# Five of eight coefficient batches on GpSimd, and a scan whose tables and products share one psum bank

## The chip, the cores and the metric

The kernel runs on one core of one Trainium2 chip. The metric is device time in microseconds (us) for one execution. Five engines matter here, each with its own in-order queue: TensorE (PE), VectorE (DVE), ScalarE (ACT), GpSimd (POOL) and SyncE (SP, which only issues DMAs). Lines such as L312 are lines of the kernel before.

## The reference, cut to what matters

Two layers of an encoder over 512 tokens of width 1024. The first layer mixes tokens with a bidirectional diagonal state-space model, the second with a short convolution; each layer then attends to 256 memory tokens and applies a squared-ReLU MLP. The part that the change touches is the state-space mixer of layer 0 and, beside it, the keys and values of layer 0's memory:

```python
u = h @ w_in                                  # 64 groups of 16 channels
for r in range(2):                            # two directions
    a_bar = exp(lam * dt)                     # 64 complex states per group
    bu = einsum('gph,lbgh->lbgp', b_bar, u)
    states = associative_scan(a_bar * left + right, bu)
    y = y + einsum('ghp,lbgp->blgh', c, states).real
z = gelu(y); z = z * sigmoid(z @ w_glu); out = z @ w_out
k, v = split(m @ w_kv)                        # memory keys and values, independent of the scan
```

## The kernel before

The tokens are cut into 64 chunks (`NC`) of 8. Inside a chunk the recurrence is a small matrix product; between chunks a scan of 63 steps carries the state. The mixer is written out by hand (`manual_schedule`): on each engine the instructions stand in the order in which the source issues them. The rest of the kernel, from about 238 us on, is left to a scheduler.

The steps of the mixer that matter here, in the order of the source:

- `s_mats(b)` (L522 to L531): TensorE makes the chunk inputs of 8 groups, ScalarE copies them into `estate`. The last of these copies must land before the scan begins, since every scan step uses all 64 groups.
- `q_ops(b)` (L535, by way of `gen_ops`, L466): five VectorE products and sums of 128x1024 that make one of eight batches `Q[b]` of the table C a^k, through a scratch page `gt`. Batches 0 to 3 stand ahead of the scan (L769), batches 4 to 7 are handed to `scan_run` as `extra` and put into the gaps between dependent scan operations.
- `scan_ops` (L594): four VectorE operations of 128x128 for each of the 63 steps, `t1 = xp*a1`, `t2 = swap(xp)*a2`, `x += t1`, `x += t2`. `a1` and `a2` lie in SBUF, and `t1` and `t2` are two separate SBUF tiles.
- `strips(i, fill)` (L545): for 16 groups, four blocks of small TensorE products of `Q[2i]` (first two blocks) and `Q[2i+1]` (last two), each followed by `fill` products of the keys and values; then ScalarE writes the page `wt`, and SP sends it to DRAM (`wd<-wt`) and reads it back as `mt` (eight `mt<-wd`).
- `y_intra(i)` (L580): the in-chunk part of the output from `mt`. `y_carry(i)` (L587) adds the carried states, which `p_part` (L660) copies out of `estate` into the tiles `pt`, the first 42 steps early and the rest after the scan.
- `kv0_gen` (L625): the keys and values of layer 0 as a generator that yields after each product; `kvp(n)` takes n of them. Eight blocks of 16 products, called kv0 to kv7 here, each accumulate in one bank from `fbank`, are copied out by ScalarE (L650, L653), and ask for the weights of the block after next on ScalarE's DMA queue.

[...] Before the change `fbank` serves two short broadcasts, kv0 to kv7 by turns, and the two tiles of `y_intra(3)`. The scan waits for nothing on TensorE; TensorE waits for the scan only by way of `p_part` and `y_carry`.

Of the kernel before, what the change touches and what calls it, by code (L numbers as in the profile page):

```python
# [12 lines left out]
F32 = mybir.dt.float32  # L13
# [6 lines left out]
P = 128  # L20
# [6 lines left out]
G = 64  # L27
# [19 lines left out]
def tile_encoder(ctx, tc, xT, xN, memT, memN, small, b_re, b_im, c_re, c_im, a_w_in, a_w_glu,  # L47
# [31 lines left out]

    # ------------------------------------------------------------------ constants  # L80
    sm = cpool.tile([P, NSM], F32, name="sm")
# [14 lines left out]

    # ------------------------------------------------------------------ weight stream
    def wblock(w, c0, k0=0):
# [71 lines left out]
    def lin_block(xs, hooks=None):  # L170
        """One 256-column block: two psum banks, accumulated over the 8 k-tiles."""
        t = next_block()
        ps = [bank([S], "lin") for _ in range(2)]
        for k in range(KT):
            if hooks and k in hooks:
                for f in hooks[k]:
                    f()
            xh, xl = xs(k)
            for m in range(2):
                mm3(ps[m], wsl(t, k, m, 0), wsl(t, k, m, 1), xh, xl, k == 0, k == KT - 1)  # L180
        return ps

    class Act2:
        """hi/lo split activation: 8 k-tiles, two per page."""

# [27 lines left out]

    # ------------------------------------------------------------------ norm helpers
    class Stats:
# [30 lines left out]

    # ================================================================== S5 phase
    man = ExitStack()
# [29 lines left out]
    def token_rstd(srcs, dst):  # L278
        """rows of tokens -> 1/rms of every token, on all partitions of dst."""
        n = len(srcs)  # L280
        ss = s5pool.tile([P, n], F32, name=nm("ss"))
        for i in range(n):
            act.activation(srcs[i], srcs[i], AF.Square, accum_out=ss[:, i:i + 1])
        act.activation(ss, ss, AF.Sqrt, scale=1.0 / D, bias=epsb)

        def rest():
            v.reciprocal(ss, ss)
            dg = page([n, P], F32, "dg")
            for i in range(n):
                act.activation(dg[:, i, :], ident, AF.Copy, scale=ss[:, i:i + 1])  # L290
            ps = fbank([n, P], "rb")
            pe.matmul(ps, lhsT=ones, rhs=dg, start=True, stop=True)
            act.copy(dst, ps.rearrange("p n q -> p (n q)"))
        return rest

    # ---- discretisation tables, [(r,p), g]
    def sm64(o):
# [29 lines left out]
    def exp_ops(o, x):  # L327
        """o = exp(x): x = n ln2 + r, polynomial in r, exponent bits from n."""
        xc, n, r, acc = t64(), t64(), t64(), t64()
# [15 lines left out]
    def merge(*lists):  # L345
        """Round-robin over independent chains."""
        lists = [list(x) for x in lists]
        while any(lists):
            for x in lists:
                if x:  # L350
                    x.pop(0)()
# [40 lines left out]
    def cmul_ops(dst, a, b, n, u):  # L392
        """dst[n,G] = a[n,G] * b[G] (complex)."""
        br, bi = bc(b[0], n), bc(b[1], n)
        return [lambda: tt(dst[0], a[0], br, ALU.mult), lambda: tt(u[0], a[1], bi, ALU.mult),
                lambda: tt(dst[1], a[0], bi, ALU.mult), lambda: tt(u[1], a[1], br, ALU.mult),
                lambda: tt(dst[0], dst[0], u[0], ALU.subtract), lambda: tt(dst[1], dst[1], u[1], ALU.add)]
# [25 lines left out]

    # per-token coefficient tables, [(r,p), g, 8]; the reverse direction runs the other way
    es = page([2, G, 8], F32, "es")
# [12 lines left out]
    x_rest = token_rstd(xn, rstd)  # L438
    a1 = cpool.tile([P, 2, G], F32, name="a1")
    a2 = cpool.tile([P, 2, G], F32, name="a2")  # L440
    dd = s5pool.tile([P, 16, 16], F32, name="dd")

    def late_tables():
        act.copy(a1[:, 0, :], pw[0][:, 8, :])
        act.copy(a1[:, 1, :], pw[0][:, 8, :])
        act.mul(a2[:, 0, :], pw[1][:, 8, :], -1.0)
        act.copy(a2[:, 1, :], pw[1][:, 8, :])
        for i in range(2):
            act.copy(eq[0:64, i], pw[i][0:64, 1:9, :].rearrange("p k g -> p g k"))
            act.copy(eq[64:128, i], pw[i][64:128, 8:0:-1, :].rearrange("p k g -> p g k"))  # L450
# [7 lines left out]

    # ---- helpers of the scan pipeline
    bb = s5pool.tile([P, 2, 65 * 16], F32, name="bb")  # L460
    nc.gpsimd.memset(bb[:, :, 64 * 16:], 0.0)
    estate = bpool.tile([P, NC, 2, G], F32, tag="big", name="estate")

    def gen_ops(b, X, xs, E, E2, flip, name):
        """8 groups of the complex products X * E, three products each; flip: the second
        operand carries -Im X and the imaginary part comes out negated."""  # L466
        g0 = 8 * b
        shape = [8, 8, 16] if flip else [8, 16, 8]
        r0, r1 = [page(shape, F32, name) for _ in range(2)]
        u = page(shape, F32, "gt")  # L470

# [15 lines left out]

    def run_ops(ops):
        for o, a, b_, op in ops:
            tt(o, a, b_, op)  # L490

# [42 lines left out]

    def q_ops(b):  # L535
        res, ops = gen_ops(b, cf, cf[2], eq, eq2, True, "Q")
        Q[b] = res
        return ops
# [4 lines left out]
    def strips(t16, fill):  # L543
        """impulse responses of 16 groups -> banded chunk matrices M[(h,j), g, (t,h')]."""
        ps0, ps1 = bank([4, T, 16], "w0"), bank([4, T, 16], "w1")  # L545
# [32 lines left out]
    def y_intra(i):  # L578
        """in-chunk part of 16 groups, rows (8 groups' half, chunk)."""
        yps[i] = [(fbank if i == 3 else bank)([4, P], "y") for _ in range(2)]  # L580
# [13 lines left out]
    def scan_ops():  # L594
        for s in range(1, NC):
            xp = estate[:, s - 1]
            x = estate[:, s]
            t1_ = s5pool.tile([P, 2, G], F32, tag="sc1", name=nm("sc1"))
            t2_ = s5pool.tile([P, 2, G], F32, tag="sc2", name=nm("sc2"))
            yield (t1_, xp, a1, ALU.mult)  # L600
# [3 lines left out]

    # ---- memory keys and values of layer 0, fp32 products
    mn = {}
# [22 lines left out]
    def kv0_gen(mp):  # L629
        """Yields after every matmul (all fp32, N = 256)."""  # L630
        for i in range(8):
# [28 lines left out]
    def p_part(b, s0, s1, engs):  # L660
        """states after steps s0..s1-1 as the carried-in states of the next chunk."""
        for ri in range(2):
# [10 lines left out]

    def p_early(b):
        p_tile(b)
        p_part(b, 0, SE, (act.copy, act.copy))

    def p_copy(b):
# [5 lines left out]

    # ---- in-projection, fp32 products, with the scan inputs pipelined behind it
    ups = {}
# [81 lines left out]
    q_tables()  # L768
    for b in range(4):  # L769
        run_ops(q_ops(b))  # L770
    kv_it = kv0_gen(mp)
    sc = list(scan_ops())
    ns = [0]

    def scan_run(n, extra=()):
        """n scan steps; the ops of extra go into the gaps between dependent ones."""
        extra = list(extra)
        for i in range(n):
            for j in range(4):
                tt(*sc[ns[0]])  # L780
                ns[0] += 1
                if j >= 2 and extra:
                    tt(*extra.pop(0))
        run_ops(extra)

    mts[0] = strips(0, 2)
    scan_run(3, q_ops(4))
    mts[1] = strips(1, 2)
    kvp(4)
    scan_run(3, q_ops(5))  # L790
    y_intra(0)
    kvp(8)
    mts[2] = strips(2, 2)
    scan_run(3, q_ops(6))
    kvp(8)
    scan_run(3, q_ops(7))
    y_intra(1)
    kvp(8)
    mts[3] = strips(3, 2)
    scan_run(3)  # L800
    scan_run(8)
    kvp(16)
    y_intra(2)
    scan_run(20)
    kvp(16)
    for b in range(4):
        p_early(b)
    kvp(48)
    scan_run(63 - 43)

    # ---- outputs: carried states through C a^k on top of the in-chunk part; gelu; to feature rows
    zf = []
# [71 lines left out]
    def norm_feed(k, st, a, vec):  # L884
        """h[k] is final for this sub-layer: statistics and the scaled hi/lo operand."""
        if a is not None:
# [3 lines left out]

    # ---- gated linear unit and out-projection
    z2 = Act2("z2")
# [23 lines left out]

    # ------------------------------------------------------------------ cross attention
    def kv_tiles():
# [89 lines left out]

    # ------------------------------------------------------------------ squared-relu MLP
    def mlp(hn_, st, vec, last):  # L1010
# [33 lines left out]
    def finish(md, r2, st):  # L1044
        """The last block, one half of the tokens after the other, each with its final norm."""
        t = next_block()
# [71 lines left out]

    # ------------------------------------------------------------------ layer 1: short conv
    cz = Act2("cz")  # L1120
# [42 lines left out]

    # ---- keys and values of layer 1
    kh, vh = kv_tiles()
# [30 lines left out]
def _layout(i):  # L1196
    """Layout only: transposes, broadcasts, padding and packing."""
    f = np.float32
# [41 lines left out]
```

## Time and profile before

| | |
|---|---|
| time, median of 3 runs | 1492.65 us (1489.86 to 1494.39) |
| span of the profiled execution, first to last instruction | 1489.2 us |
| TensorE busy in the span | 1452.9 us (98%) |
| VectorE, ScalarE, GpSimd busy | 866.4, 558.8, 2.6 us |
| granted TensorE clock, mean | 0.988 |

The page gives the profiled execution's span and no time of its own; the three times lie 0.7 to 5.2 us above that span. A busy TensorE is not TensorE at its peak. In the timelines a row with "xN" is a run of like instructions, and the bracket at its end is the idle time before it and what ended it. An fp32 product of TensorE shows as two instructions, so 16 products of a kv block are 32.

### The profile page before, as it was taken

The page shows a single profiled execution, that of the slowest core. Times are in us where ns is not written, and L with a number is a line of the kernel's source. Part 1 is how long each engine was busy: PE and PEld are TensorE (multiplying, and loading weights), DVE is VectorE, ACT ScalarE, POOL GpSimd, SP SyncE. Part 2 cuts the span into 40 slices and gives each one's busy share as a digit, 9 for nine tenths or more (in the row PEclk, how much of TensorE's full clock was granted, in tenths as well). Part 3 has the DMA queues.
Part 4 walks back from the last instruction along what each step waited for, and adds up shares of the span by engine and source line. Part 5 has one row for each costly group of instructions (what it writes and reads, how often), then busy time and mean ns, then how long its engine had stood idle before and what let it go on. Part 6 is the DMA issues. An engine that isn't in the chain of part 4 may idle for free.

```text
span 1489.2 us, 18984 instructions
## 1 busy us (share of the span) xinstructions
PE 1452.9 (98%) x7890; PEld 1200.7 (81%) x7890; DVE 866.4 (58%) x1377; ACT 558.8 (38%) x815; POOL 2.6 (0%) x25
## 2 busy tenths in 40 slices
PE   7998998999999999999999999999999999999997
PEld 3596777888888888888888888988888888888886
DVE  8877987466566444444358455546657444444435
ACT  4684166344344232231334233434445323132321
POOL 0000000000000000000000000000000000000000
PEclk9979999999999999999999999999999999999998
DMA  8613644322034323223214223622124332323201
GB/s 288 196 31 87 173 137 141 114 86 85 29 113 141 114 85 100 99 89 110 85 57 141 85 85 102 209 87 87 56 85 141 89 109 85 114 85 102 96 1 57
DMA packets 157302, 155.46 MB, mean 104 GB/s; under 512 B 11424, under 2 KB 152864, under 8 KB 157216
## 3 DMA queue, kind: packets, MB, share of 16 engines
q1 hardware_dynamic: 149888, 146.91, 31.3%
q10 hardware_dynamic: 7328, 7.34, 1.6%
q8 instruction: 62, 1.02, 0.3%
q14 instruction: 24, 0.20, 0.0%
HBM read 148.08 MB, written 6.16 MB: 104 GB/s over the span
## 4 chain that ended last, share of the span: by engine, by line
PE 90%; DVE 5%; ACT 3%; DMA 1%; issue 0%; SPq 0%; DVEq 0%; ACTq 0%
PE lin L168 25%; PE lin L166 25%; PE lin L167 25%; PE u L692 4%; PE ps_s L527 2%; DVE estate L312 1%; DVE sc L312 1%; DVE Q L312 1%; PE kv L167 1%; PE kv L168 1%; PE kv L166 1%; ACT pt L666 1%; PE tr L516 1%; ACT estate L531 1%; ACT estate L530 1%; PE sc L168 1%
## 5 line engine op out<-in xcount | busy, mean ns | idle before, releaser
L144 DVE TENSOR_TENSOR wl<-st,wh 128x1024 fp32r<-128x1024 f32 x224 | 270.7, 1222 | 171.5 <-ACT wh L143 170.8
L143 ACT CAST wh<-st 128x1024 fp32r<-128x1024 f32 x224 | 231.6, 1050 | 320.9 <-PE lin L167 293.1
L166 PE MATMUL lin<-hnh,wh 128*128 128x512 f32 x832 | 326.4, 392 | 0.0
L168 PE MATMUL lin<-hnh,wl 128*128 128x512 f32 x832 | 324.1, 390 | 0.0
L167 PE MATMUL lin<-hnl,wh 128*128 128x512 f32 x832 | 324.0, 389 | 0.0
L166 PE MATMUL lin<-mid,wh 128*128 128x512 f32 (+1 forms) x528 | 202.7, 384 | 0.0
L167 PE MATMUL lin<-mid,wh 128*128 128x512 f32 (+1 forms) x528 | 202.2, 383 | 0.0
L168 PE MATMUL lin<-mid,wl 128*128 128x512 f32 (+1 forms) x528 | 202.2, 383 | 0.0
L167 PEld LDWEIGHTS lin<-hnl,wh 128*128 128x128 f32 x832 | 156.2, 188 | 33.3 <-issue 1.2
L166 PEld LDWEIGHTS lin<-hnh,wh 128*128 128x128 f32 x832 | 156.2, 188 | 33.3 <-issue 1.2
L168 PEld LDWEIGHTS lin<-hnh,wl 128*128 128x128 f32 x832 | 156.2, 188 | 32.5
L166 PEld LDWEIGHTS lin<-mid,wh 128*128 128x128 f32 x528 | 99.3, 188 | 19.5
L167 PEld LDWEIGHTS lin<-mid,wh 128*128 128x128 f32 x528 | 99.3, 188 | 19.3
L168 PEld LDWEIGHTS lin<-mid,wl 128*128 128x128 f32 x528 | 99.2, 188 | 19.3
L312 DVE TENSOR_TENSOR relu<-relu,lin 128x512 f32<-128x512 f32 x64 | 43.7, 684 | 104.5 <-ACT relu L1024 104.5
L312 DVE TENSOR_TENSOR mo<-lin,r 128x512 f32<-128x512 f32 (+1 forms) x66 | 44.3, 675 | 102.0 <-PE lin L168 101.8
L1024 ACT ACTIVATE relu<-lin 128x512 f32<-128x512 f32 x64 | 38.1, 596 | 128.2 <-PE lin L168 127.8
L887 ACT ACTIVATE hnh<-h,sm 128x512 fp32r<-128x512 f32 x40 | 28.7, 718 | 132.0 <-DVE h L312 118.8
L692 PE MATMUL u<-xbig,st 128*128 128x512 f32 x128 | 57.6, 610 | 8.0 <-DMA st<-in_a_w_in_dram 8.0
L312 DVE TENSOR_TENSOR h<-lin,h 128x512 f32<-128x512 f32 x32 | 21.8, 692 | 67.3 <-PE lin L168 57.8
L692 PEld LDWEIGHTS u<-xbig,st 128*128 128x128 f32 x128 | 24.9, 196 | 38.4 <-issue 37.5
L1026 ACT CAST mid<-relu 128x512 fp32r<-128x512 f32 x64 | 39.5, 617 | 42.4 <-DVE relu L312 41.7
(215 smaller groups left out, 2004.0 us busy)
## 6 DMA issues: line engine op xcount, KB each, us to landing
st<-in_f_w_dram SPq DMA_DIRECT2D x64, 1024.0 KB, 5.5
st<-in_b_w_in_dram SPq DMA_DIRECT2D x12, 1024.0 KB, 5.3
st<-in_x_w_kv_dram SPq DMA_DIRECT2D x10, 1024.0 KB, 5.4
st<-in_x_w_q_dram SPq DMA_DIRECT2D x8, 1024.0 KB, 5.2
st<-in_x_w_o_dram SPq DMA_DIRECT2D x8, 1024.0 KB, 5.1
st<-in_x_w_kv_dram ACTq DMA_DIRECT2D x6, 1024.0 KB, 7.2
mt<-wd SPq DMA_DIRECT2D x32, 128.0 KB, 4.3
st<-in_a_w_glu_dram SPq DMA_DIRECT2D x4, 1024.0 KB, 5.5
```

The costliest lines, as they stand in the source:

```text
L143: act.copy(hi, src)
L144: v.tensor_tensor(out=lo, in0=src, in1=hi, op=ALU.subtract)
L166: pe.matmul(ps, lhsT=wh, rhs=xh, start=start, stop=False)
L167: pe.matmul(ps, lhsT=wh, rhs=xl, start=False, stop=False)
L168: pe.matmul(ps, lhsT=wl, rhs=xh, start=False, stop=stop)
L312: v.tensor_tensor(out=o, in0=a, in1=b, op=op)
L516: pe.transpose(ps[:, i, :], sfT[b][ri][:, g].rearrange("p h j -> p (h j)"), ident)
L527: pe.matmul(ps[:, g, :], lhsT=sf[b][ri][:, g, :], rhs=U[b // 2][:, 8 * (b % 2) + g, :], start=True, stop=True)
L692: pe.matmul(ups[i, m], lhsT=win[i][:, k, m * P:(m + 1) * P], rhs=hn[k // 2][:, k % 2, :], start=(k == 0), stop=(k == KT - 1))
L887: act.activation(a.hi(k), hk(k), AF.Copy, scale=gain(vec, k))
L1024: act.activation(r_, ps[m], AF.Relu)
L1026: act.copy(md[:, k, 0, :], r_)
```

## The change

Three things change, all in the mixer of layer 0.

- Batches 3 to 7 of `Q` are computed by GpSimd instead of VectorE: 3, 4 and 5 right behind batch 2, and 6 and 7 behind the zero fills of four `pt` tiles, which now stand ahead of the scan. All five use batch 2's scratch page `gt`.
- `a1`, `a2`, `t1`, `t2` become four slices of one psum tile `scb`, taken from `fbank` in `late_tables` and used until the last scan step. The scan's operations are written without other work between them, 42 steps and then 21.
- The hand-written order of `strips`, `kvp` and `y_intra` is changed to go with it: 64 products of the keys and values now stand behind the copies of the first 42 steps.

```diff
-    a1 = cpool.tile([P, 2, G], F32, name="a1")
-    a2 = cpool.tile([P, 2, G], F32, name="a2")
...
     def late_tables():
+        scb.append(fbank([4, 2, G], "scb"))
+        a1, a2 = scb[0][:, 0], scb[0][:, 1]
...
-    def run_ops(ops):
+    def run_ops(ops, eng=None):
         for o, a, b_, op in ops:
-            tt(o, a, b_, op)
+            (eng or v).tensor_tensor(out=o, in0=a, in1=b_, op=op)
...
-            t1_ = s5pool.tile([P, 2, G], F32, tag="sc1", name=nm("sc1"))
-            t2_ = s5pool.tile([P, 2, G], F32, tag="sc2", name=nm("sc2"))
+            a1, a2, t1_, t2_ = [scb[0][:, i] for i in range(4)]
...
-    for b in range(4):
-        run_ops(q_ops(b))
+    for b in range(3):
+        ops = q_ops(b)
+        run_ops(ops)
+    gt = ops[0][0]
+    run_ops(q_ops(3, gt), nc.gpsimd)
+    run_ops(q_ops(4, gt), nc.gpsimd)
+    run_ops(q_ops(5, gt), nc.gpsimd)
...
     mts[0] = strips(0, 2)
-    scan_run(3, q_ops(4))
+    kvp(8)
     mts[1] = strips(1, 2)
-    kvp(4)
-    scan_run(3, q_ops(5))
     y_intra(0)
     kvp(8)
     mts[2] = strips(2, 2)
-    scan_run(3, q_ops(6))
     kvp(8)
-    scan_run(3, q_ops(7))
     y_intra(1)
+    for b in range(4):
+        p_tile(b)
+    run_ops(q_ops(6, gt), nc.gpsimd)
+    run_ops(q_ops(7, gt), nc.gpsimd)
+    kvp(16)
+    mts[3] = strips(3, 2)
     kvp(8)
-    mts[3] = strips(3, 2)
-    scan_run(3)
-    scan_run(8)
-    kvp(16)
     y_intra(2)
-    scan_run(20)
-    kvp(16)
+    scan_run(SE)
     for b in range(4):
-        p_early(b)
-    kvp(48)
-    scan_run(63 - 43)
+        p_part(b, 0, SE, (act.copy, act.copy))
+    kvp(64)
+    scan_run(NC - 1 - SE)
```

In the built program the places below are where the order or the waits differ; outside the mixer, and on SP, the instructions stand as before.

VectorE before, two steps of the scan behind the last `Q` batch. `sc` are the product tiles `t1` and `t2`, `a` the coefficients; the bracket names the semaphore that an instruction waits for, and `DVE_49` is VectorE's own.

```order
L312 TENSOR_TENSOR sc_184_961<-estate,a_250 128x128 [waits DVE_49]
L312 TENSOR_TENSOR sc_185_962<-estate,a_251 128x128
L312 TENSOR_TENSOR estate<-estate,sc_184_961 128x128 [waits DVE_49]
L312 TENSOR_TENSOR estate<-estate,sc_185_962 128x128 [waits DVE_49]
L312 TENSOR_TENSOR sc_186_963<-estate,a_250 128x128 [waits DVE_49]
```

VectorE after, the end of batch 2 and the first steps of the scan. `scb` is the one psum tile.

```order
L492 TENSOR_TENSOR Q_913<-gt_914,Q_913 128x1024 [waits DVE_49]
L492 TENSOR_TENSOR scb_336<-estate,scb_336 128x128 [waits Activation_49]
L492 TENSOR_TENSOR scb_336<-estate,scb_336 128x128 [waits DVE_49]
L492 TENSOR_TENSOR estate<-estate,scb_336 128x128 [waits DMAHW7_49,DMAHW5_49,DVE_49]
L492 TENSOR_TENSOR estate<-estate,scb_336 128x128 [waits DVE_49]
L492 TENSOR_TENSOR scb_336<-estate,scb_336 128x128 [waits DVE_49] x2
L492 TENSOR_TENSOR estate<-estate,scb_336 128x128 [waits DVE_49] x2
```

Before, the second product of a step has no wait; now each operation of the scan waits for VectorE's operation ahead of it.

TensorE before, the end of `y_intra(2)`, the end of kv4 and the start of kv5 (`kv_1924`).

```order
L583 MATMUL y_1818<-mt_1531,U_478 64x128 x7
L583 MATMUL y_1819<-mt_1531,U_478 64x128 [waits Activation_49]
L583 MATMUL y_1819<-mt_1531,U_478 64x128 x7
L640 MATMUL kv_1805<-st_1612,mem_302 128x256 x4
L640 MATMUL kv_1924<-st_1803,mem_301 128x256 [waits DMAHW6_49,Activation_49]
L640 MATMUL kv_1924<-st_1803,mem_301 128x256 x3
```

TensorE after, the same place (kv5 is `kv_1816`).

```order
L585 MATMUL y_1614<-mt_1381,U_477 64x128 x7
L585 MATMUL y_1615<-mt_1381,U_477 64x128 [waits Activation_49]
L585 MATMUL y_1615<-mt_1381,U_477 64x128 x7
L641 MATMUL kv_1816<-st_1464,mem_299 128x256 [waits DMAHW4_49,DVE_49]
L641 MATMUL kv_1816<-st_1464,mem_299 128x256 x3
L641 MATMUL kv_1816<-st_1464,mem_300 128x256 x4
```

Before, kv5 waits for its weights and for ScalarE; now it waits for its weights and for VectorE. The count that it waits for is that of the last operation of the scan, the 252nd.

GpSimd after, the zero fills of the last early `pt` tile and the batch 6 (`Q_1432` and `Q_1433`); before, GpSimd has only the fills.

```order
L671 MEMSET pt_1429 64x16 [waits DMAHW4_49,PE_49,Activation_49]
L672 MEMSET pt_1429 64x16
L492 TENSOR_TENSOR gt_914<-cs_504,eq_232 128x1024 [waits Pool_49]
L492 TENSOR_TENSOR Q_1432<-cf_502,eq_15_233 128x1024 [waits DMAHW6_49,PE_49]
L492 TENSOR_TENSOR Q_1433<-cf_500,eq_16_234 128x1024 [waits DMAHW7_49,Activation_49]
L492 TENSOR_TENSOR Q_1432<-gt_914,Q_1432 128x1024 [waits Pool_49]
L492 TENSOR_TENSOR Q_1433<-gt_914,Q_1433 128x1024 [waits Pool_49]
```

The third operation of batch 6 writes a page that held `wt` of `strips(2)`, and waits for its ScalarE copy and its DMA to DRAM.

## Rows read from the trace of the kernel before

**Rows 1.** Windows by stage: us, busy time by engine, granted clock, DMA.
```profile
core 0: us, PE busy (x) PEld busy (x) DVE busy (x) ACT busy (x) POOL busy (x), PEclk, DMA share, GB/s
214.20:238.10 23.90, 19.05 (x305) 17.78 (x302) 15.25 (x30) 22.84 (x34) 0.00 (x0) 1.00 0.14 45
238.10:1489.20 1251.10, 1240.05 (x5817) 1039.24 (x5815) 666.00 (x888) 427.75 (x612) 0.00 (x0) 1.00 0.31 97
```

**Rows 2.** Timeline of VectorE, 113 to 215 us.
```profile
start us, us, engine line op out<-in xcount [idle before <-releaser]
113.10 1.22 DVE L312 TENSOR_TENSOR gt<-cs,eq 128x1024 f32<-128x1024 f32 x1
...
127.58 0.49 DVE L312 TENSOR_TENSOR sc<-estate,a 128x128 f32<-128x128 f32 x2 [8.72 <-ACT estate L531]
...
160.48 0.49 DVE L312 TENSOR_TENSOR sc<-estate,a 128x128 f32<-128x128 f32 x2
160.89 0.61 DVE L312 TENSOR_TENSOR estate<-estate,sc 128x128 f32<-128x128 f32 x2
161.54 0.49 DVE L312 TENSOR_TENSOR sc<-estate,a 128x128 f32<-128x128 f32 x2
...
213.69 0.61 DVE L312 TENSOR_TENSOR estate<-estate,sc 128x128 f32<-128x128 f32 x2
```

**Rows 3.** Timeline of TensorE, 197 to 224 us.
```profile
197.15 7.15 PE L640 MATMUL kv<-st,mem 128*128 128x256 f32 x32 [0.79 <-DMA st<-in_x_w_kv_dram]
206.52 7.15 PE L640 MATMUL kv<-st,mem 128*128 128x256 f32 x32 [2.22 <-DMA st<-in_x_w_kv_dram]
213.60 1.97 PE L583 MATMUL y<-mt,U 128*64 128x128 f32 x32
```

**Rows 4.** Timeline of ScalarE, 200 to 224 us.
```profile
200.64 0.38 ACTq L103 DMA_DIRECT2D st<-in_x_w_kv_dram  x1
...
213.70 0.58 ACT L653 COPY V<-kv 128x512 f32<-128x512 f32 x1 [8.79 <-PE kv L640]
214.31 1.66 ACT L666 COPY pt<-estate 64x168 f32<-64x168 f32 x4
```

**Rows 5.** VectorE's groups by form: count, busy us, mean ns, idle before.
```profile
L312 DVE TENSOR_TENSOR h<-h,mo 128x512 f32<-128x512 f32 x62 | 40.5, 686 | 0.3
L312 DVE TENSOR_TENSOR estate<-estate,sc 128x128 f32<-128x128 f32 x126 | 36.3, 288 | 1.8
L321 DVE SCALAR_TENSOR_TENSOR hnl<-h,sm,hnh 128x512 fp32r<-128x512 f32 x40 | 30.0, 750 | 4.6 <-ACT hnh L887 3.5
L312 DVE TENSOR_TENSOR h<-lin,h 128x512 f32<-128x512 f32 x32 | 21.8, 692 | 67.3 <-PE lin L168 57.8 <-issue 9.5
```

**Rows 6.** Windows around TensorE's wait for the first `mt`, columns as above.
```profile
139.80:146.10 6.30, 0.02 (x1) 0.00 (x0) 6.26 (x14) 0.00 (x0) 0.00 (x0) 0.90 1.00 275
146.10:151.60 5.50, 5.46 (x36) 4.81 (x37) 5.50 (x11) 0.00 (x0) 0.00 (x0) 0.50 0.46 105
```

**Rows 7.** Timeline of TensorE, 146 to 168 us.
```profile
146.13 3.68 PE L583 MATMUL y<-mt,U 128*64 128x128 f32 x32 [6.31 <-DMA wd<-wt]
149.75 4.64 PE L638 MATMUL kv<-mem,st 128*128 128x256 f32 x16
154.32 0.61 PE L553 MATMUL w<-Q,bb 64*32 64x112 f32 x32
...
156.24 0.62 PE L553 MATMUL w<-Q,bb 64*32 64x112 f32 x32
...
160.76 0.23 PE L563 MATMUL w<-dd,sm 128*32 128x16 f32 x8
...
167.34 3.72 PE L638 MATMUL kv<-mem,st 128*128 128x256 f32 x16
```

**Rows 8.** Timeline of SP: the read-back behind `strips(2)`.
```profile
166.48 7.07 SPq L573 DMA_DIRECT2D mt<-wd  x8
```

**Rows 9.** Timeline of GpSimd, its two fills of 128 partitions.
```profile
0.74 0.20 POOL L85 MEMSET ones<- 128x128 f32 x1 [0.29 <-POOLq L1230]
0.92 0.15 POOL L384 MEMSET tab<- 128x64 f32 x1
```

More of the change, by code (lines that the diff above doesn't have):

```diff
@@ L438, in tile_encoder @@
     x_rest = token_rstd(xn, rstd)
-    a1 = cpool.tile([P, 2, G], F32, name="a1")
-    a2 = cpool.tile([P, 2, G], F32, name="a2")
     dd = s5pool.tile([P, 16, 16], F32, name="dd")
+    scb = []
     def late_tables():
+        scb.append(fbank([4, 2, G], "scb"))
+        a1, a2 = scb[0][:, 0], scb[0][:, 1]
         act.copy(a1[:, 0, :], pw[0][:, 8, :])
@@ L462, in tile_encoder, with gen_ops @@
     estate = bpool.tile([P, NC, 2, G], F32, tag="big", name="estate")
-    def gen_ops(b, X, xs, E, E2, flip, name):
+    def gen_ops(b, X, xs, E, E2, flip, name, u=None):
         g0 = 8 * b
@@ L469, in gen_ops @@
         r0, r1 = [page(shape, F32, name) for _ in range(2)]
-        u = page(shape, F32, "gt")
+        u = page(shape, F32, "gt") if u is None else u
         def bx(a):
@@ L533, in tile_encoder, with q_ops @@
     Q = {}
-    def q_ops(b):
-        res, ops = gen_ops(b, cf, cf[2], eq, eq2, True, "Q")
+    def q_ops(b, u=None):
+        res, ops = gen_ops(b, cf, cf[2], eq, eq2, True, "Q", u)
         Q[b] = res
@@ L672, in p_tile @@
         pts[b] = pt
-    def p_early(b):
-        p_tile(b)
-        p_part(b, 0, SE, (act.copy, act.copy))
     def p_copy(b):
@@ L773, in tile_encoder, with scan_run @@
     ns = [0]
[L775 to L784, printed above, removed]
+    def scan_run(n):
+        run_ops(sc[ns[0]:ns[0] + 4 * n])
+        ns[0] += 4 * n
     mts[0] = strips(0, 2)
-    scan_run(3, q_ops(4))
+    kvp(8)
     mts[1] = strips(1, 2)
-    kvp(4)
-    scan_run(3, q_ops(5))
     y_intra(0)
```

## Prediction
> **What bounds the kernel now.** I read the windows by stage first. The stretch from 238.1 us to the end, 1251.1 us, is TensorE's: 1240.05 us busy at a granted clock of 1.00 [rows 1]. The change touches nothing in it, so it can only move it. What can be won or lost lies ahead of 238.1, and VectorE's timeline tells how that part ends. The scan cannot start before the last `estate` copy; VectorE stands idle for 8.72 us until 127.58 [rows 2]. From there it does 63 steps with four `Q` batches between them, and the last operation starts at about 214.0 [rows 2]. TensorE's timeline comes to the same moment by another way: kv6 runs 197.15 to 204.30, waits 2.22 us for weights, and kv7 ends at 206.52 + 7.15 = 213.67 [rows 3]. ScalarE then copies kv7 out at 213.70 and, behind that in its queue, the carried states at 214.31 [rows 4]; `y_carry` on TensorE and the 23.9 us to 238.1, with ScalarE busy for 22.84 of them [rows 1], hang on these copies. So two chains end together, VectorE's scan and TensorE's kv blocks. Making one shorter wins nothing unless the other gets shorter too, and a change that puts one behind the other pays for both.
>
> **What the change removes.** Four batches of five operations leave the stretch of the scan. In the plain part a step takes 161.54 - 160.48 = 1.06 us [rows 2], so 63 steps take 66.8 of the 86.6 us between 127.58 and 214.2: the batches cost 19.8 us there. Batch 3 went from 113.10 into time that VectorE spends idle anyway [rows 2], and its removal is worth nothing. With the step as it was the scan would end at 194.4.
>
> **What it adds to the scan.** The step is not as it was. In 1.06 us two operations are spaced by waits and two are not: `t1` and `t2` together take 160.89 - 160.48 = 0.41, that is 0.205 each, and the two sums take 0.65, that is 0.325 each, because each must see its predecessor finished [rows 2]. An operation lasts 0.288 [rows 5], so a wait adds about 0.037. Now tables and products are one tile, and every operation waits for the one ahead. A step becomes 4 x 0.325 = 1.30 us, and 252 operations take 81.9 us. From 127.58 the scan ends at 209.5, only 4.5 us sooner than before. The order of waits is certain; the 0.325 is not, because no VectorE operation in this trace writes psum. It can't go below the spacing without a wait, 0.205. For the upper end I take the largest step that another kind of operand makes: `hnl`, with a scalar from memory, 750 ns against 686 for `h<-h,mo` [rows 5], 0.064 more, so 0.389. A psum input costs nothing visible: `h<-lin,h` takes 692 ns, `h<-h,mo` 686 [rows 5]. That is the nearest row, and I keep 0.325. [...]
>
> **What waits for the scan now.** `psfill` has two banks and `scb` holds one until the last scan step. kv0 to kv4 follow each other in the other bank. Their hand-over is hidden by `strips` or `y_intra`, which stand between them, but kv5 follows without a free bank: its first product waits for the last of the 252 scan operations. Queued behind it on TensorE are kv5, kv6, kv7, `y_intra(3)` and the whole rest. Three blocks at 7.15 us [rows 3] are 21.45 us after 209.5. kv7's weights are asked for when kv5 ends and took 206.52 - 200.64 = 5.9 us [rows 3, 4], which lies inside kv6's 7.15. ScalarE's copies of the first 42 steps stand ahead of kv5's copy in its queue and run while TensorE waits. SP's first load behind the mixer waits for the end of kv6, before and now, and moves along with it.
>
> TensorE also restarts slowly. [...] I take 3.68 - 1.97 + 4.64 - 3.72 = 2.6 us for the restart at kv5. So kv7 ends at 209.5 + 21.45 + 2.6 = 233.5 instead of 213.67.
>
> **What hides the rest.** GpSimd's arithmetic is not in the trace. Its start is VectorE's end of batch 2, about 113.2 [rows 2]. From below, an operation takes the 1.22 us of VectorE's [rows 2]. The nearest GpSimd rows are the fills: 128 elements 0.20, 64 elements 0.15 [rows 9], or 0.8 us per 1024 elements; two reads and a write at that rate are 2.4, with a tenth for the start 2.5, which I take as an estimate. For the upper end I double it. At 2.5 batch 5 is there at 113.2 + 15 x 2.5 = 150.7. TensorE gets `mt` of `strips(0)` at 146.13 as before, does `y_intra(0)` and 8 kv products until 154.3, and then `strips(2)`, one of whose four blocks takes 1.92 [rows 7]: no wait. Batch 6 needs the page of that `wt`; the DMA was through at 166.48, 5.5 us after the last `w` product [rows 7, 8]. Three operations later, at 174.0, batch 6 is done, and batch 7 at 186.5. `strips(3)` does its second half behind that, 3.9 us, then 8 kv products 3.6 and `y_intra(2)` 1.97 [rows 3, 7]: TensorE stands before kv5 at 196, and waits 13.5 us for the scan. Above 3.0 us per operation batch 5 is late too, and TensorE's arrival is 130.9 + 23 times the operation; it passes 209.5 at 3.4 us. Up to there GpSimd's work costs nothing. At 5 it costs 36.
>
> **The sum.** The batches give 19.8 back, the waits in the step take 81.9 - 66.8 = 15.1, the bank takes 21.45 + 2.6 less the 0.5 by which kv7 ended ahead of the scan: 213.67 becomes 233.5, 19.8 us later. Behind kv7 ScalarE's queue is the same, so the tail moves as a whole. The span of 1489.2 becomes 1509.0. The median lies 3.45 above the span, and I add the same: 1492.65 + 19.8 = 1512.5.
>
> **Rivals.** First, not slower: psum products could be visible sooner than those in SBUF. The place is the spacing of the scan's operations. At 0.205 the scan ends at 179.2, TensorE goes from `y_intra(2)` at 196 into kv5 without a wait or a slow clock, and kv7 ends at 217.5: 1496.5, within 0.3% (4.5 us, about what a measurement tells from no change). It decides from 0.274 downward, and with a GpSimd near 1.2 us per operation it reaches 1488. Against it: a sum of before, SBUF to SBUF, lasts 0.288 without any wait, so a fall by a sixth is needed. 8%.
>
> Second, GpSimd is the bound. At 4 us TensorE is at kv5 at 222.9 and the time is 1526, at 5 us 1549. For it speaks that the products read two broadcast operands; against it the margin from 2.5 to 3.4. [...] 13%.
>
> Third, the psum operands are slower. At 0.389 the scan ends at 225.6 and the time is 1528.6. For it: VectorE writing psum is nowhere in the trace; against it the 692 against 686. 8%.
>
> Fourth, GpSimd and VectorE hinder each other while both work, from 127.6 to 186.5. If the scan stood still for all of GpSimd's operations there, about 20 x 2.5 = 50 us, the time would be 1562. In the trace GpSimd does nothing beside VectorE, so nothing speaks on either side. [...] 6%.
>
> **How the numbers follow.** The forecast has 65%: 1512.5, with its own range of 1504 to 1521 for 0.29 to 0.36 us per operation. The range from 1500 to 1532 takes it whole, the third rival and the nearer half of the second. Faster by over 0.3% needs the first rival with a fast GpSimd, 3%; within 0.3% the rest of it and a little of the forecast's edge, 6%; slower 91%.
>
> **What would show it.** In the changed profile VectorE's scan operations should start 0.32 to 0.33 us apart, all four, and end near 209.5 with nothing between them. TensorE should have one long idle stretch ahead of the first kv product behind `y_intra(2)`, released by VectorE's `estate`, then a clock of 0.50 for some us, and 3 kv blocks end to end up to 233.5. ScalarE's last `V` copy should move from 213.70 to about 233.5, with the rows behind it in the same spacing as before, and the stretch from the first `lin` product to the end should be as long as now. GpSimd's batches should be through near 186. I am wrong if the scan's spacing is under 0.27, if TensorE's wait ahead of kv5 ends on something other than VectorE, or if `strips(3)` waits for GpSimd beyond 209.5.

## The result, and the profile after

The changed kernel takes 1509.85 us (median, 1508.81 to 1510.32) against 1491.26 us of the kernel before on the same chip (1489.22 to 1494.39). The ratio is 1.0118 with a 95% interval of 1.0102 to 1.0133: slower by 18.6 us. The forecast was 1512.5, 2.6 us too high. Ratios, here and below, follow the means of the executions, and times are medians.

| | before | after |
|---|---|---|
| span of the profiled execution | 1489.2 us | 1508.1 us |
| mean granted TensorE clock | 0.988 | 0.980 |
| VectorE, ScalarE, GpSimd busy | 866.4, 558.8, 2.6 us | 850.7, 559.0, 54.2 us |
| start of the scan, start of its last two operations | 127.58, 213.69 | 126.78, 208.06 |
| end of the kv blocks (start of `y_intra(3)`) | 213.60 | 232.69 |
| first `lin` product | 238.1 | 257.25 |

Lines in the rows below are those of the changed kernel, and in an experiment's rows those of its own kernel. First the windows of the last two stages, columns as in [rows 1]:

```profile
core 0: us, PE busy (x) PEld busy (x) DVE busy (x) ACT busy (x) POOL busy (x), PEclk, DMA share, GB/s
233.35:257.25 23.90, 19.02 (x304) 17.72 (x301) 11.40 (x17) 22.83 (x34) 0.00 (x0) 1.00 0.14 45
257.25:1508.10 1250.85, 1240.26 (x5817) 1039.16 (x5815) 665.98 (x888) 427.64 (x612) 0.00 (x0) 1.00 0.31 97
```

Behind the kv blocks nothing changed: 23.90 us again, and 1250.85 us for the long stretch where [rows 1] have 1251.10. All 18.9 us of the span lie ahead of 257.25. VectorE's timeline, which answers to [rows 2], shows the scan:

```profile
start us, us, engine line op out<-in xcount [idle before <-releaser]
126.78 0.62 DVE L492 TENSOR_TENSOR scb<-estate,scb 128x128 f32<-128x128 f32 x2 [14.85 <-ACT estate L533]
127.44 0.61 DVE L492 TENSOR_TENSOR estate<-estate,scb 128x128 f32<-128x128 f32 x2
128.08 0.62 DVE L492 TENSOR_TENSOR scb<-estate,scb 128x128 f32<-128x128 f32 x2
...
207.40 0.62 DVE L492 TENSOR_TENSOR scb<-estate,scb 128x128 f32<-128x128 f32 x2
208.06 0.61 DVE L492 TENSOR_TENSOR estate<-estate,scb 128x128 f32<-128x128 f32 x2
208.59 3.77 DVE L665 COPY pt<-estate 64x168 f32<-64x168 f32 x12
```

A pair of products now takes 0.66 us where it took 0.41, a pair of sums 0.64 or 0.65 as before: a step is 128.08 - 126.78 = 1.30 us, and it is the same 1.30 beside GpSimd's work at 127 and without it at 207. TensorE's timeline, which answers to [rows 3]:

```profile
191.52 1.97 PE L585 MATMUL y<-mt,U 128*64 128x128 f32 x32
208.72 24.04 PE L641 MATMUL kv<-st,mem 128*128 128x256 f32 x96 [15.24 <-DVE estate L492]
232.69 1.97 PE L585 MATMUL y<-mt,U 128*64 128x128 f32 x32
```

TensorE stands 15.24 us for the scan's last operation and then runs kv5, kv6 and kv7 end to end. ScalarE's last `V` copy and the copies behind it have moved with them, in the spacing of [rows 4]:

```profile
232.80 0.58 ACT L654 COPY V<-kv 128x512 f32<-128x512 f32 x1 [6.32 <-PE kv L641]
233.41 1.66 ACT L667 COPY pt<-estate 64x168 f32<-64x168 f32 x4
```

The restart is as slow as in [rows 6], a granted clock of 0.50 for 5.5 us, in the window of the same columns:

```profile
208.70:214.20 5.50, 5.47 (x13) 4.35 (x14) 3.65 (x12) 0.00 (x0) 0.00 (x0) 0.50 0.00 0
```

GpSimd's arithmetic, in its timeline, of which [rows 9] had only fills:

```profile
112.10 1.93 POOL L492 TENSOR_TENSOR gt<-cs,eq 128x1024 f32<-128x1024 f32 x1 [110.90 <-ACT sf L519]
...
117.76 4.67 POOL L492 TENSOR_TENSOR Q<-gt,Q 128x1024 f32<-128x1024 f32 x2
...
165.05 1.93 POOL L492 TENSOR_TENSOR Q<-cf,eq 128x1024 f32<-128x1024 f32 x1 [14.62 <-DMA wd<-wt]
...
177.34 4.64 POOL L492 TENSOR_TENSOR Q<-gt,Q 128x1024 f32<-128x1024 f32 x2
```

A product takes 1.93 us; its two inputs are tables read with repetition. A sum of two plain pages takes 2.33. The wait for the page of `strips(2)` is where the prediction put it.

### The profile page after: what moved, and what is told of

Its sections match the earlier page's. It is cut to its first block, busy times and chain, and to the rows that moved or that the text cites. A ratio compares the mean times of both kernels' runs of the same rounds, so it can differ in the third digit from the quotient of the medians.

```text
span 1508.1 us, 18987 instructions
## 1 busy us (share of the span) xinstructions
PE 1459.4 (97%) x7890; PEld 1204.5 (80%) x7890; DVE 850.7 (56%) x1352; ACT 559.0 (37%) x815; POOL 54.2 (4%) x50
## 4 chain that ended last, share of the span: by engine, by line
PE 88%; DVE 6%; ACT 4%; issue 1%; DMA 0%; SPq 0%; DVEq 0%; ACTq 0%
PE lin L168 25%; PE lin L166 25%; PE lin L167 25%; PE u L689 3%; DVE scb L492 3%; DVE estate L492 2%; PE kv L641 2%; PE kv L168 1%; PE kv L167 1%; PE kv L166 1%; PE ps_s L529 1%; ACT estate L533 1%; ACT estate L532 1%; ACT pt L667 1%; ACT sf L519 1%
## 5 line engine op out<-in xcount | busy, mean ns | idle before, releaser
L312 DVE TENSOR_TENSOR mo<-lin,r 128x512 f32<-128x512 f32 (+1 forms) x66 | 44.2, 675 | 102.1 <-PE lin L168 101.9
```

Of the source, the lines that this page charges most:

```text
L312: v.tensor_tensor(out=o, in0=a, in1=b, op=op)
```

## The experiments

Each was timed beside the kernel before on the same chip. One thing has to be known to read the profiled executions against each other: TensorE's first 64 `ps_s` instructions, near 75 us, take 12.0 to 12.9 us in seven of the nine profiled executions, before and after among them; the granted clock over them was 0.55 in the changed kernel (73.8 to 86.7 us) and 0.55 in e7 (76.3 to 88.9). In those of e4 and e8 they take 7.36 us, at a granted clock of 1.00 (75.4 to 82.7 us in e4, 70 to 80 in e8), and all that follows starts some 5 us earlier. So scans are compared from their own start, and times by their medians.

### e1: the scan back in SBUF

```diff
-        scb.append(fbank([4, 2, G], "scb"))
-        a1, a2 = scb[0][:, 0], scb[0][:, 1]
+        a1, a2 = [cpool.tile([P, 2, G], F32, name=n) for n in ("a1", "a2")]
+        scb.append((a1, a2))
...
-            a1, a2, t1_, t2_ = [scb[0][:, i] for i in range(4)]
+            a1, a2 = scb[0]
+            t1_ = s5pool.tile([P, 2, G], F32, tag="sc1", name=nm("sc1"))
+            t2_ = s5pool.tile([P, 2, G], F32, tag="sc2", name=nm("sc2"))
```

> The changed kernel with the scan's coefficients and products in four SBUF tiles, as before the change; the five batches stay on GpSimd, and the order stays. Theory (one psum tile serialises the scan's operations and holds one of the two psum banks of the key and value blocks): the step falls from 1.30 us to about 1.06, the scan runs from 126.8 to about 193.6, and no product of the sixth key and value block (kv5) waits for it. kv5 then runs at 193.5 to 200.7; ScalarE's early pt copies (192.3 to 204.6) stand ahead of its eviction and of the asking for the last block's weights, so kv7 ends near 217.7 in place of 232.7: about 1495, 15 less than the changed kernel and about 4 over the kernel before. Rival (the scan in psum keeps GpSimd and VectorE from hindering each other, and without it they do): VectorE's scan operations or GpSimd's products get longer while both run, by a tenth or more against 0.29 and 1.93 us, and the time stays at 1505 or over.

Measured: 1505.39 us, 1.0090 of before (1.0075 to 1.0105). The rival is right in what it says of VectorE. Its timeline, from the scan's start and around the moment when GpSimd starts again:

```profile
128.24 4.12 DVE L492 TENSOR_TENSOR sc<-estate,a 128x128 f32<-128x128 f32 x2 [14.67 <-ACT estate L533]
132.29 4.44 DVE L492 TENSOR_TENSOR estate<-estate,sc 128x128 f32<-128x128 f32 x2
...
148.50 0.49 DVE L492 TENSOR_TENSOR sc<-estate,a 128x128 f32<-128x128 f32 x2
148.91 0.61 DVE L492 TENSOR_TENSOR estate<-estate,sc 128x128 f32<-128x128 f32 x2
149.56 3.95 DVE L492 TENSOR_TENSOR sc<-estate,a 128x128 f32<-128x128 f32 x2
153.43 0.61 DVE L492 TENSOR_TENSOR estate<-estate,sc 128x128 f32<-128x128 f32 x2
```

and GpSimd's beside it:

```profile
140.41 4.74 POOL L492 TENSOR_TENSOR Q<-gt,Q 128x1024 f32<-128x1024 f32 x2
145.10 0.12 POOL L673 MEMSET pt<- 64x16 f32 x1
...
149.47 1.93 POOL L492 TENSOR_TENSOR gt<-cs,eq 128x1024 f32<-128x1024 f32 x1
151.43 1.93 POOL L492 TENSOR_TENSOR Q<-cf,eq 128x1024 f32<-128x1024 f32 x1
167.11 1.93 POOL L492 TENSOR_TENSOR Q<-cf,eq 128x1024 f32<-128x1024 f32 x1 [13.75 <-DMA wd<-wt]
```

While GpSimd computes, a scan operation of 0.29 us takes about 2, the length of one of GpSimd's; between 145 and 149 and again from 153.4, where GpSimd only fills or waits, a pair takes 0.49 or 0.61. GpSimd pays almost nothing: its means go from 1927 to 1953 ns and from 2355 to 2387. The scan ends at 228.2, 100.0 us after its start, where 66.8 were expected: 33 us lost beside 18 operations of GpSimd, 1.8 each. The bank's part of the theory holds: kv5 and kv6 ran from 195.93 without a wait. kv7 then came late by another way. ScalarE's early `pt` copies, with the request for kv7's weights among them, waited until 205.01 for the 42nd step of the slowed scan, and kv7 started when the weights had landed, as TensorE's timeline shows:

```profile
219.97 9.29 PE L643 MATMUL kv<-st,mem 128*128 128x256 f32 x32 [9.97 <-DMA st<-in_x_w_kv_dram]
```

### e2: a bank of its own for the scan

```diff
-    psfill = ctx.enter_context(tc.tile_pool(name="psfill", bufs=2, space=bass.MemoryType.PSUM))
+    psfill = ctx.enter_context(tc.tile_pool(name="psfill", bufs=1, space=bass.MemoryType.PSUM))
+    psscan = ctx.enter_context(tc.tile_pool(name="psscan", bufs=1, space=bass.MemoryType.PSUM))
...
-        scb.append(fbank([4, 2, G], "scb"))
+        scb.append(sbank([4, 2, G], "scb"))
...
-        yps[i] = [(fbank if i == 3 else bank)([4, P], "y") for _ in range(2)]
+        yps[i] = [f([4, P], "y") for f in ((fbank, sbank) if i == 3 else (bank, bank))]
```

(`sbank` takes a tile from `psscan`, as `fbank` does from `psfill`.)

> The changed kernel with the scan's psum tile in a pool of its own, so that the key and value blocks have one psum bank alone and never one that the scan held; the scan's operations and their waits stay, so the scan still ends near 208.6. Theory (the sixth block kv5 stands for 15.24 us because the scan's tile holds one of its two banks until the last scan operation): kv5 no longer waits, runs at 193.5 to 200.7, its eviction comes behind ScalarE's pt copies at about 205.2, kv6 runs to 212.4 and kv7 from about 213.1 to 220.3 in place of 232.7: about 1497.5, 12 less than the changed kernel. Rival (kv5 stands for something that the scan computes and not for its bank): the wait of about 15 us stays and the time is 1509.9, or more for the one bank.

Measured: 1500.91 us (1493.03 to 1501.78), 1.0043 of before (1.0025 to 1.0061): 9 less than the changed kernel, where 12 were expected. TensorE's timeline:

```profile
191.88 7.17 PE L645 MATMUL kv<-st,mem 128*128 128x256 f32 x32
203.91 10.03 PE L645 MATMUL kv<-st,mem 128*128 128x256 f32 x32 [4.86 <-ACT V L658]
...
222.47 1.97 PE L589 MATMUL y<-mt,U 128*64 128x128 f32 x32 [0.68 <-ACT V L658]
```

kv5 waits for nothing, though the scan's step is 1.30 us as in the changed kernel and its last operation ends at 209.5: the 15.24 us were the bank's, not the state's. The 4.86 us ahead of kv6 are the eviction that stands behind ScalarE's `pt` copies, as expected; the restart after it (10.03 in place of 7.17) was not in the expectation and is 2.9 of the 3.4 us by which the time lies above it.

### e3: tables in psum, products in SBUF

```diff
-            a1, a2, t1_, t2_ = [scb[0][:, i] for i in range(4)]
+            a1, a2 = [scb[0][:, i] for i in range(2)]
+            t1_ = s5pool.tile([P, 2, G], F32, tag="sc1", name=nm("sc1"))
+            t2_ = s5pool.tile([P, 2, G], F32, tag="sc2", name=nm("sc2"))
```

> The changed kernel with the coefficients left in the psum tile and the two products of each step in two SBUF tiles, so that the two multiplications read psum and write SBUF, and the two sums read SBUF alone. Theory (it is the waits of one tile that make a step 1.30 us, four times 0.325, not the place of the operands): the second multiplication and the first sum no longer wait for the operation ahead, the step is about 1.06 us as before the change, the scan ends near 193.6 and the coefficients' bank comes free there; kv7 ends near 217.7: about 1495. Rival (a psum operand makes an operation slower): the multiplications stay longer than before the change, the step lies between 1.15 and 1.30 and the scan ends at 199 to 208: 1500 to 1509.

Measured: 1535.81 us, 1.0288 of before (1.0266 to 1.0311). Both theories miss the time by over 25 us, and the timeline says why more sharply than e1 does:

```profile
129.03 0.48 DVE L492 TENSOR_TENSOR sc<-estate,scb 128x128 f32<-128x128 f32 x2 [15.03 <-ACT estate L533]
129.44 3.35 DVE L492 TENSOR_TENSOR estate<-estate,sc 128x128 f32<-128x128 f32 x2
132.82 0.49 DVE L492 TENSOR_TENSOR sc<-estate,scb 128x128 f32<-128x128 f32 x2
133.22 3.93 DVE L492 TENSOR_TENSOR estate<-estate,sc 128x128 f32<-128x128 f32 x2
...
222.83 0.48 DVE L492 TENSOR_TENSOR sc<-estate,scb 128x128 f32<-128x128 f32 x2
223.23 0.61 DVE L492 TENSOR_TENSOR estate<-estate,sc 128x128 f32<-128x128 f32 x2
```

Side by side, in the same microseconds and beside the same GpSimd operations, the products (one input from psum) run 0.48 a pair, as fast as in [rows 2], and the sums (two inputs from SBUF) take 3.35 and 3.93. What stops VectorE here is two SBUF inputs. Without GpSimd a step is 1.05 us, 1.06 in [rows 2], so a table read from psum cost nothing. e3 takes away the waits of the one tile and the products in psum together, so by itself it doesn't say which of them made up the 0.24; the mean of a product does, 295 ns into psum in the changed kernel and 288 into SBUF in the kernel before:

```profile
L312 DVE TENSOR_TENSOR sc<-estate,a 128x128 f32<-128x128 f32 x126 | 31.0, 288 | 10.6 <-ACT estate L531 8.7
```

Two products a step make 0.014 of that, so the waits are nearly all of the 0.24. The large loss in e3 is the bank again. In this build kv4 gets the scan's bank, and TensorE stands in the middle of `strips(3)` until the scan's last product has read its table, as its timeline shows:

```profile
223.37 2.08 PE L643 MATMUL kv<-st,mem 128*128 128x256 f32 x4 [42.59 <-DVE sc L492]
```

### e6: the psum tile alone

The kernel before with the tables and products in `scb`, and nothing else changed.

```diff
-    a1 = cpool.tile([P, 2, G], F32, name="a1")
-    a2 = cpool.tile([P, 2, G], F32, name="a2")
...
+        scb.append(fbank([4, 2, G], "scb"))
+        a1, a2 = scb[0][:, 0], scb[0][:, 1]
...
-            t1_ = s5pool.tile([P, 2, G], F32, tag="sc1", name=nm("sc1"))
-            t2_ = s5pool.tile([P, 2, G], F32, tag="sc2", name=nm("sc2"))
+            a1, a2, t1_, t2_ = [scb[0][:, i] for i in range(4)]
```

> The kernel before with one part of the change alone: the scan's coefficients and products in one psum tile of the two banks; all eight batches stay on VectorE where they were, and so does the order. Here the key and value blocks all get the other bank, and only the last in-chunk part needs the scan's bank. Theory (the one tile adds 0.24 us a step, and nothing hinders it): the scan's plain steps are 1.30 us apart, it ends 15 us later than before, near 229 in place of 214, TensorE's kv blocks end near 215 and wait there, and the time is about 1507, 15 over the kernel before. Rival (psum operands cost more when SBUF-bound batches stand between them, or the kv blocks wait for the bank too): 1515 or over. A result under 1500 would say that the bank's loss alone made the changed kernel slow.

Measured: 1509.42 us, 1.0117 of before (1.0102 to 1.0131), 2 over the expectation. The scan went from 129.49 to 231.6, 102.1 us in place of 86.6: the 15 expected. The kv blocks did not end near 215, and there the rival was right that they wait for the bank too. With one bank left, kv6 waited 19.25 us for kv5's eviction, which stood behind the `pt` copies of 42 steps, and kv7 ended at 233.8, 2 us behind the scan. TensorE's timeline:

```profile
216.03 9.88 PE L641 MATMUL kv<-st,mem 128*128 128x256 f32 x32 [19.25 <-ACT V L654]
```

So the psum tile alone costs 18 us, GpSimd and the new order without it (e1) cost 13, and all together 18.6 and not 31. With the psum tile GpSimd's help is real: the scan takes 81.9 us in the changed kernel and 102.1 in e6. But kv5 then waits for the bank until the scan's end, with kv6 and kv7 behind it.

### e4: psum as long as GpSimd works, and another order

The psum tile has a bank of its own and serves the first 24 steps; then SBUF tables and products take over, and kv4 and kv6 use the bank. GpSimd gets three batches in place of five, since VectorE has time for two in its wait for `estate`. The order is written anew around it (only its core is shown).

```diff
-            a1, a2, t1_, t2_ = [scb[0][:, i] for i in range(4)]
+            if s <= SP:
+                a1, a2, t1_, t2_ = [scb[0][:, i] for i in range(4)]
+            else:
+                a1, a2 = as_
+                t1_ = s5pool.tile([P, 2, G], F32, tag="sc1", name=nm("sc1"))
+                t2_ = s5pool.tile([P, 2, G], F32, tag="sc2", name=nm("sc2"))
...
-            ps = fbank([2, ML], "kv")
+            ps = (sbank if i in (4, 6) else fbank)([2, ML], "kv")
...
+    kvp(4)
     y_intra(0)
-    kvp(8)
+    run_ops(q_ops(7, gt), nc.gpsimd)
+    kvp(4)
...
     mts[3] = strips(3, 2)
+    scan_run(NC - 1 - SE)
+    for b in range(2):
+        p_part(b, 0, SE, (act.copy, act.copy))
     kvp(8)
+    for b in range(2, 4):
+        p_part(b, 0, SE, (act.copy, act.copy))
     y_intra(2)
...
+    kvp(16)
...
+    kvp(8)
+    pump_dma(2)
+    y_carry(0)
+    yt = y_evac(0)
+    kvp(8)
```

> A version meant to beat both. The psum tile has a bank of its own and serves the first 24 scan steps alone, as long as GpSimd works; the other 39 steps use the four SBUF tiles of the kernel before. Batches 3 and 4 run on VectorE in the 13 us in which it waits for the last estate copies, batches 5 to 7 on GpSimd. kv products fill TensorE's waits for mt and Q, ScalarE's early pt copies are spread between the kv evictions, and the carried part of the first 32 groups is computed ahead of the second half of the last kv block. Theory (two SBUF inputs are what stops VectorE while GpSimd works, and the single psum tile costs 0.24 us a step): GpSimd works from 125 to 157 at 1.93 and 2.33 us an operation; the scan takes 24 x 1.30 = 31 us to 158 and 39 x 1.06 = 41 us to 199; the kv blocks end at 205 to 210, and the first lin product stands at 226 to 232, where it stood at 238.1 before the change: 1479 to 1487. Rival (the gain is taken by ScalarE or by the pages behind the last kv block): the first lin product stays within 3 us of 238 and the time within 1489 to 1495.

Measured: 1480.09 us (1473.11 to 1481.29), 0.9913 of before (0.9895 to 0.9931): by the medians 11 us faster than before and 30 faster than the change. By the means it is 13 faster than before, since two of the six executions took 1473 and 1475. VectorE's timeline at the hand-over, with GpSimd's last operation ending at 154.3:

```profile
123.97 0.62 DVE L498 TENSOR_TENSOR scb<-estate,scb 128x128 f32<-128x128 f32 x2 [1.00 <-ACT estate L539]
...
153.90 0.62 DVE L498 TENSOR_TENSOR scb<-estate,scb 128x128 f32<-128x128 f32 x2
154.56 0.61 DVE L498 TENSOR_TENSOR estate<-estate,scb 128x128 f32<-128x128 f32 x2
155.20 0.49 DVE L498 TENSOR_TENSOR sc<-estate,a 128x128 f32<-128x128 f32 x2
155.61 0.61 DVE L498 TENSOR_TENSOR estate<-estate,sc 128x128 f32<-128x128 f32 x2
...
196.26 1.78 DVE L676 COPY pt<-estate 64x168 f32<-64x168 f32 x8
```

The scan takes 31.2 us for 24 steps and 41.1 for 39. TensorE's longest wait between the scan's start and the first `lin` product, at 222.19, is 1.32 us. From its timeline:

```profile
180.60 17.53 PE L652 MATMUL kv<-st,mem 128*128 128x256 f32 x80
198.06 3.71 PE L598 MATMUL y<-Q,pt 128*64 128x128 f32 x64
...
222.19 0.50 PE L170 MATMUL lin<-zsh,wh 128*128 128x512 f32 x1 [1.32 <-ACT wh L147]
```

The start at 222.19 holds the 5 us by which this execution is ahead from the first `ps_s` instructions on; without them it lies in the 226 to 232 that were expected.

### e7 and e8: what the order, GpSimd and psum are worth

e7 is e4 with batches 5 to 7 on VectorE in the scan's gaps and an SBUF scan, so the order alone, with e4's banks and with batch 4 ahead of the scan; e8 is e4 with the SBUF scan beside GpSimd. The edits are against e4.

```diff
-    SE, SP = 42, 24
+    SE, SP = 42, 0
...
-    scan_run(SE)
+    scan_run(SE, q_ops(5, gt) + q_ops(6, gt) + q_ops(7, gt))
```

(The first pair of lines is all of e8; e7 has both, and its GpSimd computes no batch.)

> The version that beat both kernels, with its order of work, but without either part of the change: GpSimd does no batch, the scan stays in its four SBUF tiles, and batches 5 to 7 lie on VectorE between the first scan steps, as in the kernel before. It tells how much of the 11 us came from the order and how much from GpSimd and psum. Theory (both count): the scan takes 63 x 1.06 + 15 x 1.0 = 82 us in place of 72, the carried part that stood at 198.1 waits for it until about 207, and TensorE can't fill that: about 1488, 8 over the full version and 4 under the kernel before. Rival (the order is all of it): 1478 to 1482, no different from the full version.

> The version that beat both kernels, with batches 5 to 7 on GpSimd and the whole scan in its four SBUF tiles: the psum steps alone are undone. It prices what two SBUF inputs cost VectorE beside GpSimd. Theory (one scan operation gets through for each of GpSimd's 15 operations): in GpSimd's 31 us the scan gets 15 operations done, under 4 steps of 63; the other 59 take 62.5 us, so it ends about 94 us after its start in place of 72, the carried part and all behind it come 20 us later: about 1500, 8 over the kernel before. Rival (the two engines only share the time, each slowed in proportion to its work): GpSimd's operations get longer by a tenth, the scan ends 80 us after its start, 1488.

Measured: e7 1489.13 us, 0.9975 of before (0.9966 to 0.9984); e8 1499.01 us, 1.0037 (1.0023 to 1.0050). Both theories hold within 1.2 us, and both rivals fall. From the scan's start to the first late `pt` copy it is 72.3 us in e4, 210.62 - 129.09 = 81.5 in e7 and 217.15 - 123.90 = 93.2 in e8. e7's VectorE timeline has

```profile
129.09 0.49 DVE L316 TENSOR_TENSOR sc<-estate,a 128x128 f32<-128x128 f32 x2 [3.15 <-ACT estate L539]
...
210.62 1.78 DVE L676 COPY pt<-estate 64x168 f32<-64x168 f32 x8
```

In e8's VectorE timeline 16 operations of the scan lie between 123.90 and 155.02:

```profile
123.90 3.14 DVE L498 TENSOR_TENSOR sc<-estate,a 128x128 f32<-128x128 f32 x2 [1.03 <-ACT estate L539]
126.96 4.38 DVE L498 TENSOR_TENSOR estate<-estate,sc 128x128 f32<-128x128 f32 x2
...
150.23 4.79 DVE L498 TENSOR_TENSOR estate<-estate,sc 128x128 f32<-128x128 f32 x2
155.05 0.49 DVE L498 TENSOR_TENSOR sc<-estate,a 128x128 f32<-128x128 f32 x2
```

GpSimd's 15 operations lie between 123.03 and 154.87: one scan operation gets through for each of them. By the medians the order alone is 3 us faster than the kernel before and e4 9 faster than the order alone; GpSimd without psum (e8) loses 10 against the order alone.

## Why the prediction was right

**The step.** 252 operations at 0.325 us were forecast to take 81.9 us; from 126.78 to 208.67 they took 81.9. The place of the operands adds next to nothing to it: 295 ns for a product into psum against 288 into SBUF in the kernel before, and in e3 a step with psum tables is 1.05 us. The scan began 0.8 us earlier than the sum assumed, and that 0.8 is most of the difference between 233.5 and the measured 232.7 for the end of kv7.

**The bank.** kv5 waited for the last scan operation, as forecast, and e2 took the wait away by giving the scan another bank. The wait was 15.24 us and not 13.5, since GpSimd was faster than estimated and TensorE stood there at 193.5 instead of 196. That changes nothing, because both lie ahead of the scan's end.

**The three blocks and the restart.** 21.45 + 2.6 = 24.05 was forecast, 24.04 measured. The four terms of the 2.6 are `y_intra` (3.68) and 16 kv instructions (4.64) behind the 6.3 us wait, after which [rows 6] have a granted clock of 0.50, and the same work later (1.97 and 3.72) [rows 3, 7]. At kv5 the granted clock was 0.50 for 5.5 us, 0.94 in the 5.8 us behind them and 1.00 from 220 us on.

**GpSimd.** 2.5 us an operation was the estimate, 1.93 and 2.33 (mean 2.10) the measurement; batch 7 was through at 182.0 instead of 186.5. TensorE waited for it in `strips(3)` for 2.16 and 1.88 us, inside the time that it would have stood before kv5 anyway. The second rival's bound of 3.4 us was not near.

**The sum.** 213.67 to 233.5, +19.8, was forecast; the first `lin` product moved by 257.25 - 238.1 = 19.1. In the wording of the sum one sign is wrong: the 0.5 us by which kv7 ended ahead of the scan has to be added (24.05 + 0.5 + 15.1 - 19.8 = 19.85), and "less the 0.5" would give 18.85. The forecast itself was worked out from 233.5 and has it right. Of the 2.6 us between 1512.5 and the time, 1.4 are the kernel before, which took 1491.26 here and 1492.65 in the prediction.

**The rivals.** The first falls: psum products are visible no sooner; the operation behind one starts 0.33 us after it (0.66 a pair), where an SBUF sum has 0.325 (0.65 a pair in [rows 2]). The third falls: the products, whose output is in psum, have a mean of 295 ns, and the sums 286, where [rows 5] have 288. VectorE's groups by form:

```profile
L492 DVE TENSOR_TENSOR scb<-estate,scb 128x128 f32<-128x128 f32 x126 | 37.2, 295 | 19.2 <-ACT estate L533 14.8
L492 DVE TENSOR_TENSOR estate<-estate,scb 128x128 f32<-128x128 f32 x126 | 36.1, 286 | 4.3
```

**The fourth rival** was the one to weigh more carefully. In the changed kernel the two engines do not hinder each other: a step is 1.30 us beside GpSimd and without it, and a pair of GpSimd's sums takes 4.67 us at 117.76, when VectorE is idle, and 4.64 at 177.34, beside the scan. That is so only because every scan operation has an input from psum: beside GpSimd a pair with two SBUF inputs took 4.12 and 4.44 us in e1, and in e3 the sums, with two, took 3.35 a pair and the products, with one, 0.48. Of the 50 us that the prediction gave for a scan that stands still beside 20 operations, e1 lost 33 beside 18, each shorter than the estimate.

The prediction had no row in which both engines work, and kept its forecast. It did not say that the psum tile, which it counted as a cost alone, is what makes GpSimd's help possible; e1, e3 and e8 show that.

**What stays open.** Which kv block gets the scan's bank differs between builds (kv5 in the changed kernel, kv4 in e3, none in e6), and no run was made to find what decides it.

## What to carry to other kernels

Before work goes from VectorE to GpSimd, look at what VectorE does meanwhile: here operations with two SBUF inputs stood still for the length of a GpSimd operation each (about 2 us in place of 0.29 in e1), and one operand in psum freed them (0.48 a pair in e3). The one tile that the scan's dependent operations shared made each wait for the one ahead (1.30 us a step against 1.06), and it held one of two rotating banks and stopped the kv blocks that rotate there (15.24 us in the changed kernel, 42.59 in e3), so use psum for as long as GpSimd works and no longer. And when two chains end together, shortening one is not enough: in the changed kernel GpSimd took 20 us off the scan and nothing off the time of e6, and in e4, where the order around the scan was changed too, GpSimd and psum were worth 9. Whether e4's bank and its hand-over after 24 steps would have done without the new order was not tested.

## What the runs showed of the hardware

- A VectorE operation of 128x128 with two SBUF inputs took about 2 us beside GpSimd instead of 0.29 (a pair 4.12 and 4.44 us in e1, 3.35 and 3.93 in e3, 2.54 to 4.79 in e8), about one per GpSimd operation: 16 beside 15 in e8. With one psum input it took 0.286 and 0.295 (the changed kernel), a pair 0.48 beside GpSimd (e3). GpSimd's own operations grew by 1 to 2% only (1927 ns in the changed kernel, 1953 in e1, 1969 in e8).
- GpSimd's fp32 128x1024 product of two tables read with repetition took 1.93 us and its sum of two plain pages 2.33 (the changed kernel); VectorE took 1.22 for either (the kernel before, mean 1220 ns). All the products have such inputs and none of the sums, so no run tells whether the operation or its inputs make the difference.
- The spread of some kernels' times (1493 or 1501 for e2, 1473 or 1480 for e4) is as large as the 5.4 us by which the first 64 `ps_s` instructions differ between executions, 7.36 us at a granted clock of 1.00 in e4, or 12.73 in e7, where the clock was 0.50 from 80 to 90 us. That it is the cause was not tested.
